# A Fourier layer folded by symmetry: map rows folded in the feed-forward before, tokens folded beside the root, the map ended half by half

## The chip, the cores and the metric

The kernel runs on one core of a Trainium2 chip. The metric is the device time of one execution in microseconds. Engines are named as in the profile: PE is TensorE (matmuls, with PEld its weight loads), DVE is VectorE, ACT is ScalarE, POOL is GpSimd, SP is SyncE, whose queue issues most DMAs.

## The reference

A two-layer encoder on 512 tokens of 1024 channels, in fp32. Layer 0 mixes tokens by differential attention and a gated linear recurrence; layer 1 by a Fourier transform. Each mixer and each feed-forward stands between two RMS norms:

```python
def fourier_mixer(h, w):
    B, S, D = h.shape
    g = h.astype(jnp.float32).reshape(B, S, FOURIER_GROUPS, FOURIER_GROUP_DIM)
    f = jnp.fft.fft2(g, axes=(1, 3), norm='ortho').real
    return f.reshape(B, S, D).astype(h.dtype) @ w

def swiglu(h, wg, wu, wd):
    return (jax.nn.silu(h @ wg) * (h @ wu)) @ wd
...
    for l in range(DEPTH):
        ...
        x = x + rmsnorm(m, ln_mix_post[l])
        hn = rmsnorm(x, ln_ffn_pre[l])
        x = x + rmsnorm(swiglu(hn, w_ffn_gate[l], w_ffn_up[l], w_ffn_down[l]), ln_ffn_post[l])
```

There are 4 channel groups of 256 channels. The real part of a 2-D transform over positions and channels is cos(position) x cos(channel) - sin(position) x sin(channel), so both transforms are matmuls with constant matrices. `dft_pos` holds 257 cosine columns and 255 sine columns; `dft_ch` the cosine and sine matrix of one group.

## The kernel before

**Arithmetic.** Each fp32 operand is held as a high and a low part (`split`, L99 to L106: a cast on ScalarE, L103, then a subtraction on VectorE, L106). `mm3` (L108 to L111) multiplies two such pairs with three matmuls. Matmuls are 512 or about 256 columns wide.

**Weights.** All large weights are a list of 85 units of 1 MB, read in order by SP as two 512 KB halves into three raw buffers (`raw`), cast and split into pairs (`whi`, `wlo`) by `prep_half`. Units 48 to 51 are the Fourier layer's map, 52 to 84 the second feed-forward: 52 gate, 53 up, 54 gate, 55 up, and so on. For units in `LO_POOL` GpSimd, not VectorE, makes the low part. `next_unit(ahead)` hands out a unit and prepares those up to `ahead` further. A raw buffer is free for the next load when its low part is made. All pairs, activations and constants share 33 tiles of 4 KB a partition (tag `t`); when none is free, the instruction that would fill one waits for the last reader of an older one. PSUM has 8 banks of 512 columns.

**Stages.** Layer 0's mixer, its feed-forward (`ffn(0, ...)`), the Fourier layer, the second feed-forward. `ffn` runs 11 passes u, each with a gate and an up unit (`col_tiles`, matmuls `pc`), then the down projection `proj_tok` (matmuls `pj`), which takes the pairs of gated activations (`gs`) as moving operand and finishes the four blocks of 128 tokens one after the other; its last six pairs of weights a token are 36 matmuls. `finish` normalises a block while TensorE is at the next: `post_norm` (sum of squares on ScalarE, a one-column power on GpSimd, multiply-adds on VectorE), then `after`.

**The Fourier layer before.** `after0` calls `pre_norm_tok`: the root mean square (`pre_stats`), then high and low part of the whole normalised block (L788, L789), token rows on partitions. `load_dft`, a hook in the down projection, loads `dft_pos` on GpSimd's queue into 8 half tiles. `pos_dft(c, ks)` transforms over positions for one of 8 blocks of 128 channels (`put`, 12 matmuls of 512); the first six blocks run with the first three tokens, then take the fourth. The channel gain is applied as the result is split (`u`, L836, L837). `ch_dft(c)` transforms over channels (`pe`, `po`, 12 matmuls of about 256 a block), and `mirror` makes the full 512 positions from the even and odd half (L864, L865). The map is a `proj_tok` over 8 blocks of rows (192 matmuls of 512), whose `fin1` finishes a token block as its columns are done; `turn_x` transposes the normalised block and splits it into `hnhi`, `hnlo` for the feed-forward. The transposes of the last two blocks are put off into the feed-forward's first pass (`deferred`), which runs 256 tokens at a time (`halves`).

**Order.** Each engine runs its instructions in the order in which they stand in its queue, and waits at the first whose operands or buffers aren't ready. That order is fixed when the kernel is built, by a scheduler that mostly follows the order of the code.

## Time and profile before

| | |
|---|---|
| time, median of 3 runs | 1051.09 us (1050.26 to 1052.09) |
| the profiled execution's own time | 1050.92 us |
| its span | 1049.1 us |
| mean granted TensorE clock | 0.994 |
| PE busy | 1031.0 us (98%) |
| DVE, ACT, POOL busy | 477.8, 382.1, 96.2 us |
| first matmul of the Fourier layer | 600.35 us after the span's start |
| first matmul of the feed-forward behind it | 679.00 us |

The span runs from the first to the last instruction of the profiled execution; its time also has what lies around the span. The marks are starts of single instructions in the timeline. A group of the profile names line, engine, operation, output and inputs, and shapes; behind the bars stand busy time, the mean of one in ns, and the idle time of the engine ahead of it with what ended it. Line numbers are those of the kernel before, unless a row is from the changed one.

### The profile page before, as it was taken

The numbers are of one execution on the slowest core, as the hardware profiler recorded it, in microseconds if no ns is written. First come the engines' busy times: TensorE is split into PE (matmuls) and PEld (weight loads), VectorE is DVE, ScalarE is ACT, GpSimd is POOL, SyncE is SP. The second block draws the span as 40 slices with busy tenths as digits, with TensorE's granted clock in tenths as the row PEclk, the third lists the DMA queues.
The fourth block names the chain that finished last, engine by engine and source line by source line (L and its number), as shares of the span: only waits on it lengthen the run. The fifth ranks groups of instructions, "written<-read, shape, count | busy, mean of one in ns | idle before, by whom it ended". The sixth has DMA issues, their size and how long they took to land.

```text
span 1049.1 us, 12316 instructions
## 1 busy us (share of the span) xinstructions
PE 1031.0 (98%) x4959; PEld 857.8 (82%) x4959; DVE 477.8 (46%) x723; ACT 382.1 (36%) x629; POOL 96.2 (9%) x94
## 2 busy tenths in 40 slices
...
GB/s 224 124 93 115 104 41 81 143 19 63 234 105 111 120 90 81 81 119 82 141 142 80 3 88 131 6 89 207 113 115 93 81 81 120 81 80 138 3 1 81
DMA packets 72982, 102.41 MB, mean 98 GB/s; under 512 B 3879, under 2 KB 61276, under 8 KB 72925
## 3 DMA queue, kind: packets, MB, share of 16 engines
...
q10 hardware_dynamic: 578, 1.05, 0.3%
...
## 4 chain that ended last, share of the span: by engine, by line
PE 88%; DVE 6%; ACT 3%; issue 1%; DMA 1%; POOL 1%; SPq 0%; POOLq 0%; DVEq 0%; ACTq 0%
PE pc L110 15%; PE pc L109 15%; PE pc L111 15%; PE pj L111 10%; PE pj L110 10%; PE pj L109 10%; DVE p L588 1%; DVE p L582 1%; ACT whi L103 1%; PE pT L251 1%; ACT p L93 1%; PE pqk L109 1%; DVE aT L106 1%; DMA raw<-in_w_in_dram 1%; PE put L109 1%
## 5 line engine op out<-in xcount | busy, mean ns | idle before, releaser
L106 DVE TENSOR_TENSOR wlo<-raw,whi 128x1024 fp32r<-128x1024 f32 x158 | 192.2, 1241 | 273.1 <-ACT whi L103 222.0
L110 PE MATMUL pc<-hnlo,whi 128*128 128x512 f32 (+1 forms) x768 | 285.1, 372 | 0.0
L109 PE MATMUL pc<-hnhi,whi 128*128 128x512 f32 (+1 forms) x768 | 284.6, 372 | 0.5 <-ACT hnhi L103 0.5
L111 PE MATMUL pc<-hnhi,wlo 128*128 128x512 f32 (+1 forms) x768 | 284.9, 371 | 0.0
L103 ACT CAST whi<-raw 128x1024 fp32r<-128x1024 f32 x164 | 167.9, 1050 | 117.5 <-PE pj L110 31.1
L110 PEld LDWEIGHTS pc<-hnlo,whi 128*128 128x128 f32 x768 | 144.7, 188 | 25.5 <-DVE hnlo L106 0.4
L109 PEld LDWEIGHTS pc<-hnhi,whi 128*128 128x128 f32 x768 | 144.2, 188 | 26.0 <-ACT hnhi L103 1.0
L111 PEld LDWEIGHTS pc<-hnhi,wlo 128*128 128x128 f32 x768 | 144.7, 188 | 24.6
L109 PE MATMUL pj<-whi,gs 128*128 128x512 f32 x352 | 136.9, 389 | 0.0
L110 PE MATMUL pj<-wlo,gs 128*128 128x512 f32 x352 | 136.9, 389 | 0.0
L111 PE MATMUL pj<-whi,gs 128*128 128x512 f32 x352 | 136.9, 389 | 0.0
L93 ACT ACTIVATE gated<-pc 128x512 f32<-128x512 f32 x44 | 26.2, 597 | 271.8 <-PE pc L111 271.8
L749 DVE TENSOR_TENSOR gated<-gated,pc 128x512 f32<-128x512 f32 x44 | 30.2, 687 | 112.7 <-PE pc L111 112.7
L109 PEld LDWEIGHTS pj<-whi,gs 128*128 128x128 f32 x352 | 66.1, 188 | 13.8
L111 PEld LDWEIGHTS pj<-whi,gs 128*128 128x128 f32 x352 | 66.1, 188 | 13.7
L110 PEld LDWEIGHTS pj<-wlo,gs 128*128 128x128 f32 x352 | 66.1, 188 | 13.6
L217 POOL TENSOR_TENSOR r<-m,mhalf 128x1 f32<-128x1 f32 x32 | 17.5, 548 | 543.3 <-DVE m L216 536.8
L262 ACT ACTIVATE junk<-pj 128x512 f32<-128x512 f32 x32 | 19.2, 599 | 94.9 <-DVE y L261 57.8
L261 DVE TENSOR_TENSOR y<-pj,gpost 128x512 f32<-128x512 f32 x32 | 22.0, 689 | 56.6 <-PE pj L111 56.5
L103 ACT CAST gs<-gated 128x512 fp32r<-128x512 f32 x44 | 25.3, 618 | 52.1 <-PE pj L110 32.2
L106 DVE TENSOR_TENSOR gs<-gated,gs 128x512 fp32r<-128x512 f32 x44 | 28.4, 686 | 31.3 <-ACT gs L103 31.3
L93 ACT ACTIVATE p<-p,mn 128x512 f32<-128x512 f32 x32 | 22.9, 719 | 31.1 <-DVE mn L582 27.9
(193 smaller groups left out, 1261.2 us busy)
## 6 DMA issues: line engine op xcount, KB each, us to landing
raw<-in_w_ffn_gate_dram SPq DMA_DIRECT2D x44, 512.0 KB, 3.9
raw<-in_w_ffn_up_dram SPq DMA_DIRECT2D x44, 512.0 KB, 4.9
raw<-in_w_ffn_down_dram SPq DMA_DIRECT2D x44, 512.0 KB, 3.5
raw<-in_w_in_dram SPq DMA_DIRECT2D x20, 512.0 KB, 4.4
raw<-in_w_mix_out_dram SPq DMA_DIRECT2D x8, 512.0 KB, 3.3
raw<-in_w_fourier_out_dram SPq DMA_DIRECT2D x8, 512.0 KB, 3.7
pos<-in_dft_pos_dram POOLq DMA_DIRECT2D x8, 256.0 KB, 5.5
...
```

The lines of the kernel that those rows point to most:

```text
L93: ins = A.activation(out_, in_, func, **kw)
L103: A.copy(hi, src)
L106: lo_eng.tensor_tensor(out=lo, in0=src, in1=f(hi), op=ALU.subtract)
L109: T.matmul(ps, lhsT=l[0], rhs=r[0], start=start, stop=False)
L110: T.matmul(ps, lhsT=l[0], rhs=r[1], start=False, stop=False)
L111: T.matmul(ps, lhsT=l[1], rhs=r[0], start=False, stop=stop)
L217: G.tensor_tensor(out=r, in0=m, in1=mhalf[:, 0:1], op=ALU.pow)
L251: T.transpose(pt[:, k * P:(k + 1) * P], xh[:, k * P:(k + 1) * P], ident)
L261: V.tensor_tensor(out=ys[h], in0=ps[h], in1=g[:, h * S:(h + 1) * S], op=ALU.mult)
L262: A.activation(junk, ps[h], AF.Square, scale=RD, accum_out=ss[h])
L582: last_score[0] = V.tensor_tensor_reduce(out=pr[m], in0=ps[m], in1=bias[h][:, 384 - t * P:384 - t * P + S], op0=ALU.add, op1=ALU.min, scal ...
L749: V.tensor_tensor(out=gated[fc], in0=gated[fc], in1=ps, op=ALU.mult)
```

## The change

The Fourier layer is written anew around symmetries. With even and odd combinations of channels c and 256-c only half of the channel matrix is needed, and with even and odd combinations of the map's rows j and 256-j of each group the mirrored channel outputs never have to be made.

- **Tokens.** `pre_norm_tok` multiplies a block by the gain, adds and subtracts the reversed channels of each group, and scales the folded block by the root as it is split. The blocks 2 and 3 of x are stored to DRAM (`scratch`) and gathered back with reversed rows, since the second half of the tokens now comes out mirrored.
- **Map rows.** `fold_w`, called in passes 1 to 4 of layer 0's feed-forward, loads 128 rows of a group, gathers the reversed other half, adds and subtracts, and stores both to DRAM (`wfold`), from which units 48 to 51 are read.
- **The rest.** Channel 128 of each group goes through `pos_rest`, `ch_rest` and a row tile `w128`/`wr`; token 256 through `acc`, four multiply-adds with rows of `wfold`.
- **The transforms.** `pos_dft` works on halves of about 256 columns, `ch_dft` has 8 matmuls a group, the map 104 matmuls in two halves of the tokens (`map_part`, `map_rest`), each ended by `map_out`.
- **The feed-forward behind.** Its first pass (`wide`) takes three weight units (two passes' gate, one up) by halves of the tokens; the transposes of the last two blocks all come between the halves. Units 48, 50, 52 and 54 join `LO_POOL`.
- **The start and the end.** Index rows for the gathers are made on GpSimd at the start; two of the four output blocks go out by a scatter.

```diff
-LO_POOL = (8,9,10,11,12,13)
+LO_POOL = (8,9,10,11,12,13,48,50,52,54)
...
+    def fold_w(g):
+        a, b, c = (tile1k("fold") for _ in range(3))
+        nc.sync.dma_start(a, w_fourier_out[g * 256:g * 256 + P, :])
+        gather(b, w_fourier_out, rowx["w%d" % g])
+        G.memset(b[0:1, :], 0.0)
+        V.tensor_tensor(out=c, in0=a, in1=b, op=ALU.add)
+        V.tensor_tensor(out=a, in0=a, in1=b, op=ALU.subtract)
+        for z, w in enumerate((c, a)):
+            G.dma_start(wfold[g * 256 + z * P:g * 256 + (z + 1) * P, :], w)
...
-                    if deferred and (h == 1 or c == P):
+                    if deferred and (h == 1 or c == P) and not (late and h == 0):
                         deferred.pop(0)()
+                while late and deferred:
+                    deferred.pop(0)()
...
+        if wide:
+            ug, uu, vg = next_unit(2), next_unit(1), next_unit(0)
+            col_tiles([(ug, 0), (ug, P), (uu, 0), (uu, P), (vg, 0), (vg, P)],
+                      lambda i, ps: consume(i, ps, 0) if i < 4 else consume(i - 4, ps, 1), True, True)
+            vu = next_unit(3)
+            col_tiles([(vu, 0), (vu, P)], lambda i, ps: consume(i + 2, ps, 1), False)
...
     def pre_norm_tok(t):
+        r = pre_stats(t, [junk, junk])
+        h = tile1k("h")
+        V.tensor_tensor(out=h, in0=xt[t], in1=g_pre1[0], op=ALU.mult)
...
+        V.tensor_tensor(out=wv[:, 0, :, 1:P], in0=hv[:, :, 1:P], in1=hv[:, :, 255:P:-1], op=ALU.add)
+        V.tensor_tensor(out=wv[:, 1, :, 1:P], in0=hv[:, :, 1:P], in1=hv[:, :, 255:P:-1], op=ALU.subtract)
...
+        for z in range(2):
+            sl = slice(z * S, (z + 1) * S)
+            A.activation(hi[:, sl], w[:, sl], AF.Copy, scale=r)
+            V.scalar_tensor_tensor(out=lo[:, sl], in0=w[:, sl], scalar=r, in1=f(hi[:, sl]), op0=ALU.mult, op1=ALU.subtract)
...
     def after0(t):
...
+        if t >= 2:
+            nc.sync.dma_start(scratch[(t - 2) * P:(t - 1) * P, :], xt[t])
...
             posT.append([])
+            for z in range(2):
+                w = tile1k("pos", F32R)
+                G.dma_start(w[:, 0:257], dft_pos[z, k * P:(k + 1) * P, 0:257])
+                G.dma_start(w[:, 258:513], dft_pos[z, k * P:(k + 1) * P, 257:512])
...
+    w128 = tile1k("w128")
+    G.memset(w128, 0.0)
+    for q in range(3):
+        nc.sync.dma_start(w128[32 * q:32 * q + 4, :], w_fourier_out.rearrange("(g j) d -> g j d", j=256)[:, P, :])
+    wr = tile1k("wr", F32R)
+    A.copy(wr, w128)
...
+    for g in range(4):
+        pos_dft(g, (0, 1, 2))
+    pos_rest((0, 1, 2))
+    prep_one()
+    pos_rest((3,))
...
+    for g in range(4):
+        ch_dft(g)
+    ch_rest()
+    gather(xr[1], scratch, rowx["c"])
+    gather(xr[2], scratch, rowx["d"])
...
+    for g in range(4):
+        raw = raws.tile([P, 1024], F32, name=nm("raw"), tag="raw")
+        nc.sync.dma_start(raw, wfold[g * 256:g * 256 + P, :])
...
+            V.scalar_tensor_tensor(out=acc, in0=raw, scalar=e256[g], in1=acc, op0=ALU.mult, op1=ALU.add)
...
+    split(acch, accl, acc)
...
+    def map_out(i):
+        y = [pair("ya"), pair("yc")]
+        for h in range(2):
+            A.copy(y[0][h], psm[i][1][h])
+            V.tensor_tensor(out=y[1][h], in0=psm[i][0][h], in1=y[0][h], op=ALU.add)
+            V.tensor_tensor(out=y[0][h], in0=psm[i][0][h], in1=y[0][h], op=ALU.subtract)
+        for z in range(2):
+            t = (z, 3 - z)[i]
+            post_norm(t, y[z], g_post1, G if z else V)
+            pre_norm(t, g_fpre1)
...
+    wf = [next_unit(2)]
+    for i in range(2):
+        for h in range(2):
+            map_part(i, h, 0)
+    wf += [next_unit(2), next_unit(2), next_unit(2)]
+    for h in range(2):
+        for g in (1, 2, 3):
+            map_part(0, h, g)
+        map_rest(0, h)
+    map_out(0)
...
+    turn_x(0)
+    turn_x(1)
+    map_out(1)
+    deferred.extend((lambda: turn_x(2), lambda: turn_x(3)))
...
-    ffn(1, after1, 4)
+    ffn(1, after1, 4, wide=True)
```

Where instructions now stand. First GpSimd's queue around the last token block of layer 0's feed-forward; `r` is the root of a mean square, `ch` the channel matrix. Before:

```order
78 L217 TENSOR_TENSOR r_4699<-m_4698,mhalf 128x1
79 L116 DMA gpre_5103<-in_ln_ffn_pre_dram 128x1024
80 L217 TENSOR_TENSOR r_4750<-m_4749,mhalf 128x1
81 L819 DMA ch_4769<-in_dft_ch_dram 128x1024
82 L217 TENSOR_TENSOR r_4763<-m_4762,mhalf 128x1
83 L819 DMA ch_4771<-in_dft_ch_dram 128x1024
84 L217 TENSOR_TENSOR r_5232<-m_5231,mhalf 128x1
85 L217 TENSOR_TENSOR r_5245<-m_5244,mhalf 128x1
```

After; `wlo` are low parts of unit 48, `x_816` and `x_817` the gathered blocks, `w_818` is w128:

```order
164 L117 DMA gpost_5181<-in_ln_mix_post_dram 128x1024
165 L251 TENSOR_TENSOR r_4898<-m_4897,mhalf 128x1
166 L117 DMA gpre_5183<-in_ln_ffn_pre_dram 128x1024
167 L251 TENSOR_TENSOR r_4910<-m_4909,mhalf 128x1
168 L107 TENSOR_TENSOR wlo_4928<-raw_4925,whi_4927 128x1024
169 L199 DMA x_816_4937<-scratch,ixc 128x1024
170 L107 TENSOR_TENSOR wlo_4934<-raw_4931,whi_4933 128x1024
171 L945 MEMSET w_818_4939 128x1024
172 L199 DMA x_817_4938<-scratch,ixd 128x1024
```

The memset of w128 stands behind both low parts and the first gather, where before only DMA issues stood behind the last root. Next ScalarE's queue at the same place, from the last block's squares on. Before, with `hnhi` the last block's high part and `u` the split position transforms:

```order
340 L223 ACTIVATE junk_4756,ss_4757<-x_82 128x512
341 L223 ACTIVATE junk_4756,ss_4758<-x_82 128x512
342 L788 ACTIVATE hnhi_4562<-x_82,r_4763 128x1024
343 L836 ACTIVATE u_4836<-put_4773,vcols 128x512
344 L836 ACTIVATE u_4842<-put_4783,vcols 128x512
345 L836 ACTIVATE u_4848<-put_4793,vcols 128x512
346 L836 ACTIVATE u_4854<-put_4803,vcols 128x512
347 L836 ACTIVATE u_4860<-put_4813,vcols 128x512
```

After, with `wr_4944` the cast of w128 and `whi_5036`, `whi_5042` the halves of unit 49:

```order
336 L257 ACTIVATE junk,ss_4904<-x_84 128x512
337 L257 ACTIVATE junk,ss_4905<-x_84 128x512
338 L104 CAST whi_4927<-raw_4925 128x1024
339 L104 CAST whi_4933<-raw_4931 128x1024
340 L846 ACTIVATE hnhi_4688<-w_4916,r_4910 128x512 x2
341 L949 CAST wr_4944<-w_818_4939 128x1024
342 L104 CAST whi_5036<-raw_5034 128x1024
343 L104 CAST whi_5042<-raw_5040 128x1024
344 L104 CAST u_5049<-put_5024 128x258
345 L104 CAST u_5058<-put_4948 128x512
346 L104 CAST u_5067<-put_4967 128x512
347 L104 CAST u_5076<-put_4986 128x512
```

Between the last block's high part and the first u now stand the cast of w128 and two weight casts. Last, ScalarE's queue at the end of the map. Before, with `pj` the map's sums and `whi` the weights of units 52 and 53:

```order
377 L103 CAST f_5093<-oy_5066 128x512
378 L103 CAST f_5098<-oy_5088 128x512
379 L103 CAST whi_5165<-raw_5163 128x1024
380 L103 CAST whi_5171<-raw_5169 128x1024
381 L103 CAST whi_5183<-raw_5181 128x1024
382 L103 CAST whi_5189<-raw_5187 128x1024
383 L262 ACTIVATE junk,ss_5224<-pj_5107 128x512
384 L262 ACTIVATE junk,ss_5225<-pj_5108 128x512
```

After, with `pm` the map's sums, `acc` the values of token 256, `whi_5215` to `whi_5257` units 50 and 51, `whi_5263` to `whi_5281` units 52 and 53:

```order
357 L992 CAST fr_4947<-pe_5164 128x256
358 L104 CAST acc_5201<-acc_5187 128x1024
359 L104 CAST whi_5215<-raw_5213 128x1024
360 L104 CAST whi_5221<-raw_5219 128x1024
361 L104 CAST whi_5251<-raw_5249 128x1024
362 L104 CAST whi_5257<-raw_5255 128x1024
363 L104 CAST whi_5263<-raw_5261 128x1024
364 L104 CAST whi_5269<-raw_5267 128x1024
365 L104 CAST whi_5275<-raw_5273 128x1024
366 L104 CAST whi_5281<-raw_5279 128x1024
367 L1043 COPY ya_5327<-pm_5207 128x512
368 L1043 COPY ya_5327<-pm_5208 128x512
```

All four casts of the feed-forward's weights, and ahead of them the casts of acc and the map's own, stand in front of the two copies that begin the first half's output.

More of the change, by code (lines that the diff above doesn't have):

```diff
@@ L188, in prep_one @@
         prep_half()
+    last_unit = [len(units)]
     def next_unit(ahead=3):
@@ L192, in next_unit @@
         consumed[0] += 1
-        while emitted[0] <= i + ahead and emitted[0] < len(units):
+        while emitted[0] <= i + ahead and emitted[0] < last_unit[0]:
             prep_one()
@@ L736, in drain, with ffn @@
         count[0] += 1
-    def ffn(l, after, tail, hook=None):
+    def ffn(l, after, tail, hook=None, wide=False, early=None):
         gated = [None] * NF
@@ new lines, in encoder_kernel, with pos_dft @@
+    last_unit[0] = len(units) - 4 - NF // 2 * 3
+    ffn(0, after0, 6, load_dft, early=lambda u: fold_w(u - 1) if 0 < u < 5 else None)
+    last_unit[0] = len(units)
+    prep_one()
+    xr = [xt[0], xpool.tile([P, D], F32, name=nm("x2"), tag="x2"), xpool.tile([P, D], F32, name=nm("x3"), tag="x3"), xt[1]]
+    ups = {}
+    def pos_dft(g, ts):
+        if g not in ups:
+            ups[g] = bank("put")
+        ps = ups[g]
+        for t in ts:
+            for z, (r0, o0, n) in enumerate(((0, 0, 258), (257, 256, 256))):
+                o = (z * 4 + g) * P
+                mm3(ps[:, o0:o0 + n], [a[:, o:o + P] for a in hf[t]], [a[:, r0:r0 + n] for a in posT[t]],
+                    t == 0 and z == 0, t == 3 and z == 1, skip_group_check=True)
@@ new lines, in pos_rest, with take_u @@
+    def pos_rest(ts):
+        if "r" not in ups:
+            ups["r"] = bank("put")
+        ps = ups["r"]
+        for t in ts:
+            mm3(ps[:, 0:258], [a[:, S:2 * S:4] for a in hf[t]],
+                [a[:, 0:258] for a in posT[t]], t == 0, t == 3)
+    uts = {}
+    def take_u(g):
+        uts[g] = pair("u", F32R)
+        split(*uts[g], ups[g])
+    w128 = tile1k("w128")
+    G.memset(w128, 0.0)
+    for q in range(3):
+        nc.sync.dma_start(w128[32 * q:32 * q + 4, :], w_fourier_out.rearrange("(g j) d -> g j d", j=256)[:, P, :])
@@ new lines, in encoder_kernel @@
+    wr = tile1k("wr", F32R)
+    A.copy(wr, w128)
+    V.tensor_tensor(out=wr[32:64, :], in0=w128[32:64, :], in1=f(wr[32:64, :]), op=ALU.subtract)
+    fr = tile1k("fr", F32R)
+    for g in range(4):
+        pos_dft(g, (0, 1, 2))
+    pos_rest((0, 1, 2))
+    prep_one()
+    pos_rest((3,))
+    uts["r"] = pair("u", F32R)
+    split(*[a[:, 0:258] for a in uts["r"]], ups["r"][:, 0:258])
+    for g in range(4):
+        pos_dft(g, (3,))
+        take_u(g)
+    fe, fo, e256 = [None] * 4, [None] * 4, {}
@@ new lines, in ch_dft @@
+    def ch_dft(g):
+        pe, po = bank("pe"), bank("po")
+        ut, ur = uts[g], uts["r"]
+        mm3(pe[:, 0:258], (chw(0), chw(1)), [a[:, 0:258] for a in ut], True, False)
+        for a in ur:
+            T.matmul(pe[:, 0:258], lhsT=chw(4 + g), rhs=a[:, 0:258], start=False, stop=a is ur[1])
+        mm3(po[:, 0:256], (chw(2), chw(3)), [a[:, 256:512] for a in ut], True, True)
+        eo = tile1k("feo", F32R).rearrange("p (n k) -> p n k", k=256)
+        e, o = fe[g], fo[g] = (eo[:, 0, :], eo[:, 1, :]), (eo[:, 2, :], eo[:, 3, :])
+        split(*[a[:, 0:256] for a in e], pe[:, 0:256])
+        e256[g] = sm("e256")
+        V.tensor_copy(e256[g], pe[:, 256:257])
+        for a in o:
+            G.memset(f(a[:, 0:1]), 0.0)
+        split(*[a[:, 1:256] for a in o], po[:, 1:256])
@@ new lines, in ch_rest @@
+    def ch_rest():
+        ps = bank("pe")
+        n = 0
+        for g in (0, 1, 2, 3, "r"):
+            for a in uts[g]:
+                T.matmul(ps[:, 0:258], lhsT=chw(8 + (4 if g == "r" else g)), rhs=a[:, 0:258], start=n == 0, stop=n == 9)
+                n += 1
+        e256["r"] = sm("e256")
+        V.tensor_copy(e256["r"], ps[:, 256:257])
+        A.copy(fr[:, 0:256], ps[:, 0:256])
+        V.tensor_tensor(out=fr[64:P, 0:256], in0=ps[64:P, 0:256], in1=f(fr[64:P, 0:256]), op=ALU.subtract)
@@ L876, in encoder_kernel @@
+    for g in range(4):
+        ch_dft(g)
+    ch_rest()
+    gather(xr[1], scratch, rowx["c"])
+    gather(xr[2], scratch, rowx["d"])
     g_post1 = gbc(ln_mix_post, 1, "gpost")
```

171 lines of the change are left out of this document (94 added, 77 removed).

## The prediction

> **What bounds the kernel now.** I read the page first: the busy shares and the chain of work that ended last.
>
> ```profile
> PE 1031.0 (98%) x4959; PEld 857.8 (82%) x4959; DVE 477.8 (46%) x723; ACT 382.1 (36%) x629; POOL 96.2 (9%) x94
> ...
> PE 88%; DVE 6%; ACT 3%; issue 1%; DMA 1%; POOL 1%; SPq 0%; POOLq 0%; DVEq 0%; ACTq 0%
> ```
>
> TensorE is busy 98% of the span and holds 88% of the chain. Then the stage that is rewritten: the waits of TensorE from 560 to 760 us, and its busy time by stage (columns: length, then busy time and instructions of PE, PEld, DVE, ACT, POOL, then clock, DMA share, GB/s).
>
> ```profile
> PE pc L109 <- ACT hnhi L103: 0.2, 1, 0.2
> ...
> 560.00:600.35 40.35, 40.35 (x180) 33.42 (x178) 18.00 (x34) 14.47 (x34) 3.27 (x6) 1.00 0.09 32
> 600.35:633.66 33.31, 33.31 (x193) 29.52 (x192) 20.43 (x35) 18.32 (x35) 2.76 (x5) 1.00 0.30 86
> 633.66:677.20 43.54, 43.54 (x203) 36.21 (x202) 25.57 (x49) 18.19 (x42) 3.27 (x6) 1.00 0.21 68
> ```
>
> In 200 us TensorE waits 0.2 us. From 600.35 to 677.20 it is never idle, while VectorE is busy 20.43 + 25.57 = 46 of 77 us. So before, this stage is worth what its matmuls cost. Their paces and the marks of the stage, from the timeline (start, duration):
>
> ```profile
> 600.35 0.39 PE L109 MATMUL put<-pos,hnhi 128*128 128x512 f32 x1
> 600.58 0.39 PE L110 MATMUL put<-pos,hnhi 128*128 128x512 f32 x1
> ...
> 679.00 0.28 PE L109 MATMUL pc<-hnhi,whi 128*128 128x256 f32 x1
> 679.11 0.28 PE L110 MATMUL pc<-hnlo,whi 128*128 128x256 f32 x1
> 679.23 0.28 PE L111 MATMUL pc<-hnhi,wlo 128*128 128x256 f32 x1
> ...
> 731.93 0.60 ACT L93 ACTIVATE gated<-pc 128x512 f32<-128x512 f32 x1 [5.28 <-PE pc L111]
> ```
>
> A 512-wide matmul takes 0.2267 us (0.23, to more places over a run of them), a 256-wide one 0.12. The layer starts at 600.35, the next feed-forward at 679.00, and that one's third pair of weights (u=2) at 731.93 less 24 x 0.2267 = 726.5.
>
> **The change part by part.** *TensorE's own work.* Before: 96 + 192 matmuls 512 wide and 96 about 256 wide: 288 x 0.2267 + 96 x 0.12 = 76.8 us. After: 96 + 12 + 42 about 256 wide and 104 of 512: 150 x 0.12 + 104 x 0.2267 = 41.6. The wide first pass adds 96 matmuls of 0.12 and drops 48 of 0.2267: +0.6. If TensorE never waited, the change would be worth -34.6 us. The question is how much of that becomes waiting. I follow the waits link by link in the order the changed program has, on the clock of before, with these durations (VectorE, ScalarE and GpSimd groups with their mean ns; then DMA landings):
>
> ```profile
> L106 DVE TENSOR_TENSOR wlo<-raw,whi 128x1024 fp32r<-128x1024 f32 x158 | 192.2, 1241 | 273.1 <-ACT whi L103 222.0
> L103 ACT CAST whi<-raw 128x1024 fp32r<-128x1024 f32 x164 | 167.9, 1050 | 117.5 <-PE pj L110 31.1
> L217 POOL TENSOR_TENSOR r<-m,mhalf 128x1 f32<-128x1 f32 x32 | 17.5, 548 | 543.3 <-DVE m L216 536.8
> L262 ACT ACTIVATE junk<-pj 128x512 f32<-128x512 f32 x32 | 19.2, 599 | 94.9 <-DVE y L261 57.8
> L261 DVE TENSOR_TENSOR y<-pj,gpost 128x512 f32<-128x512 f32 x32 | 22.0, 689 | 56.6 <-PE pj L111 56.5
> L103 ACT CAST gs<-gated 128x512 fp32r<-128x512 f32 x44 | 25.3, 618 | 52.1 <-PE pj L110 32.2
> L106 DVE TENSOR_TENSOR gs<-gated,gs 128x512 fp32r<-128x512 f32 x44 | 28.4, 686 | 31.3 <-ACT gs L103 31.3
> ...
> L106 POOL TENSOR_TENSOR wlo<-raw,whi 128x1024 fp32r<-128x1024 f32 x12 | 29.2, 2441 | 26.8 <-ACT whi L103 26.8
> L494 POOL TENSOR_TENSOR gate<-gate,xc 128x512 f32<-128x512 f32 x8 | 12.3, 1560 | 40.0 <-ACT gate L93 40.0
> ...
> L532 POOL TENSOR_TENSOR gate<-gate,gate 128x512 f32<-128x512 f32 x4 | 5.4, 1346 | 17.6 <-DVE c L586 17.6
> L810 POOL DMA_DIRECT2D pos<-in_dft_pos_dram x4 | 2.1, 537 | 0.0
> masks.py:197 POOL MEMSET ident<- 128x128 f32 x1 | 0.2, 206 | 0.3 <-POOLq L935 0.3
> L935 POOL MEMSET const-float32-1.0<- 128x1 f32 x1 | 0.1, 99 | 0.0
> ...
> raw<-in_w_ffn_gate_dram SPq DMA_DIRECT2D x44, 512.0 KB, 3.9
> raw<-in_w_ffn_up_dram SPq DMA_DIRECT2D x44, 512.0 KB, 4.9
> raw<-in_w_fourier_out_dram SPq DMA_DIRECT2D x8, 512.0 KB, 3.7
> raw<-in_w_mix_out_dram SPq DMA_DIRECT2D x8, 512.0 KB, 3.3
> out_dram<-x SPq DMA_DIRECT2D x4, 256.0 KB, 2.0
> vrows<-in_conv_w_dram SPq DMA_DIRECT2D x1, 8.0 KB, 4.4
> ```
>
> *In layer 0's feed-forward.* The folds add 8 VectorE adds of 1.24 (10 us over four passes) and GpSimd DMAs to engines that are mostly idle there: nothing; without that cover, 10 us. The eight wider position tiles take shared tiles in the down projection. In three places a pair of activations is now split one or two matmuls ahead of its use: 0.62 + 0.69 less that cover leaves about 0.7, three times: **+2.2** (0 to 3.9).
>
> *The wait for row 128 (w128).* The last token's statistics stand here before:
>
> ```profile
> 602.90 1.41 DVE L266 SCALAR_TENSOR_TENSOR x<-y,r,x 128x512 f32<-128x512 f32 x2 [0.69 <-POOL r L217]
> ...
> 605.42 0.56 POOL L217 TENSOR_TENSOR r<-m,mhalf 128x1 f32<-128x1 f32 x1 [2.02 <-DVE m L216]
> ```
>
> The gain multiply (1.24) now stands ahead of that m on VectorE, and the folds make a token cost VectorE slightly more than the 36 x 0.2267 = 8.16 us in which TensorE makes one (0.2): the pow ends at 605.42 + 0.56 + 1.24 + 0.2 = 607.4. Behind it GpSimd has a weight's low part (2.44), the gather of a row-reversed token, another low part (2.44), and the 128x1024 memset. The memset's price is 0.1 + 8 x 0.1 = 0.9 from the two memset rows. The gather has no row: its issue is between 0.5 (the plain DMA) and 2.4 (the longest row); 1.0, nearer the plain DMA. So the memset ends at 614.2. Only then may SP's three small loads go; they land after 2.0 to 4.4, I take the middle, 3.2: 617.4. ScalarE holds the cast wr for that, and behind it, in order, stand two weight casts and all casts of u: 1.05 + 2 x 1.05 + about 1.0 gives the first group's u at 621.6, and its low part, behind wr's and two weights' on VectorE, at 623.3. TensorE's 108 position matmuls end at 600.35 + 108 x 0.12 = 613.3. It idles 8.3 us, then 1.6. The 42 channel matmuls end at 623.3 + 5.0 = 628.3.
>
> *The clock after an idle stretch.* The trace has one such stretch (layer 0), in the timeline and in windows:
>
> ```profile
> 175.61 0.39 PE L110 MATMUL poT<-aT,v 128*128 128x256 f32 x1 [3.02 <-DVE aT L106]
> ...
> 176.00:179.00 3.00, 3.00 (x16) 2.67 (x17) 1.95 (x8) 2.13 (x6) 0.00 (x0) 0.51 0.38 145
> 179.00:182.00 3.00, 3.00 (x15) 2.19 (x16) 2.46 (x6) 2.51 (x5) 1.53 (x1) 0.92 0.01 3
> ```
>
> After 3.02 us without a matmul the granted clock is 0.51 and 0.92: 3 x 0.49 + 3 x 0.08 = 1.7 us lost. The idle 8.3 us will do the same, on the path: **+1.7**. The later idle stretch before the feed-forward does it too, but the waits inside that pass take it up. A third gap, of about 3 us (below), lies at this row's length: by the row another 1.7 (1059.4), which I leave to the range since transposes run in it. The Trainium skill, page "TensorE: Matmul & The Clock Gate", section "What's actually happening", puts the change to half clock after an idle window of some 3.4 us; by it that third gap is free and the sum stays 1057.7. The trace's 3.02 us speaks for an earlier point.
>
> *The map.* All four products with token 256's values (acc) wait for the last channel matmul. From 628.3 one chain runs through the three raw buffers: a multiply 1.24, a load into the freed buffer 3.7, two multiply-adds 2 x 1.24, acc's cast and a weight's cast 2.1, two GpSimd low parts 4.9 (units 50 and up are now GpSimd's), a load 3.9, cast 1.05, GpSimd 2.44, a load 4.9, cast 1.05: 27.8 us, to 656.1, about 0.4 more with issue times: 656.5. ScalarE's copies that begin the first half's output stand behind that last cast, which serves the next layer. TensorE's 104 matmuls need 23.6 us, wait 4.4 in between and end at about 656.3.
>
> *The first half's output.* From 656.5: copies and adds 3, squares 1.6, m and pow 0.8, x 1.4, squares 1.4, pow 0.9 (behind token 1's two multiplies, 2 x 1.56, on GpSimd), normalised token 1.4: 667.0. Token 1 repeats all from its squares on, 7.0, of which 0.5 overlaps; turned and split, 1.3. The feed-forward's first matmul comes at **674.8**, after 18.5 us with little but transposes; before, 679.00.
>
> *The wide pass.* 288 x 0.12 = 34.6. Its third pair's weights (unit 54) are cast behind the second half's activations on ScalarE and GpSimd: waits of about 2.8 + 2.0 + 1.3 = 6.1. Tokens 2 and 3 are then turned all at once, uncovered: 3. So it ends at 718.5; 48 x 0.2267 = 10.9 for unit 55 gives 729.4 for u=2, against 726.5: **+2.9**. Start (index rows, under an idle GpSimd) and scattered output: nothing (up to 1).
>
> **The sum:** 2.2 + 1.7 + 2.9 = +6.8 on the profiled execution's 1050.92 us (span 1049.1, 1.8 around it), 0.17 under the median shown: **1057.7 us**. The waits are 2.2 + 9.9 + 1.7 + 4.4 + 18.5 + 9.1 = 45.8 us, against the 34.6 saved and 4.5 of transposes and small waits that before has between the same marks beside its matmuls.
>
> **The rivals.**
> 1. *The wide pass doesn't wait* (faster). If unit 54's casts slip ahead of their use, 9 us go: 1048.7. It decides on unit 54: with under 2.3 us of waits in that pass the time equals before's. Against: its casts stand behind the second half's on two engines in order. For: the first half's chain may be late, and then the second half's matmuls are all done. Chance 0.12.
> 2. *All waits at their low ends*: no wide-pass waits (9), none in the feed-forward of layer 0 (2.2), the small loads after 2.0 and the gather 0.5 (1.7), the map's three loads after 3.3 (2.6), GpSimd's multiplies 1.35 (0.4): 1041.8. For: VectorE has slack in every window above. Against: the chains go by order, not by load. Chance 0.20.
> 3. *Longer waits*: the small loads take 4.4 (1.2), the gather 2.4 (1.4), a third clock loss (1.7), another 1.5 in the map: 1063.5. Chance 0.14.
> 4. *TensorE keeps its 98%*: 1016.3. The orders on ScalarE speak against it. Chance 0.03.
>
> **How the numbers follow.** Forecast 0.45 (its own range 1052 to 1063); the four rivals 0.49; 0.06 for a sum that comes to nothing. A measurement of this kernel tells 0.2%, 2.1 us, from no change. Faster: rivals 2 and 4 and two thirds of 1: 0.31. Same: the rest of 1 and the nothing, 0.09. Slower: 0.60. The range runs from rival 2 to rival 3, 1041 to 1064.
>
> **What would show it.** Right: a wait of TensorE near 613 us for u that the trace puts down to ScalarE, of 8 to 10 us, with wr's cast just before; a clock near 0.5 after it; ScalarE's copies of the map directly behind the cast of an up weight; some 18 us of idle before the first pc matmul; waits in the wide pass for ScalarE and GpSimd. Wrong: u cast before 616, the copies before 650, or a wide pass of under 37 us.

## The result, and the profile after

The changed kernel takes 1065.86 us (median of 4 runs, 1065.57 to 1067.09) against 1051.57 for the kernel before: a ratio of 1.0140, interval 1.0125 to 1.0155, some 14.3 us slower. The forecast was 1057.7 us, 6.6 over the median shown there. The direction is right; the forecast change is less than half of the measured one. Of the times below, that of experiment 2 leaves out one execution of 2033.85 us, far from the other three.

The page of the changed kernel, busy shares and chain:

```profile
PE 1011.1 (95%) x4877; PEld 841.3 (79%) x4877; DVE 500.4 (47%) x741; ACT 378.5 (36%) x621; POOL 165.0 (15%) x217
...
PE 77%; DVE 11%; ACT 4%; POOL 3%; issue 3%; DMA 1%; POOLq 0%; DVEq 0%; SPq 0%; ACTq 0%
```

TensorE is busy 20 us less in a span that is 16 us longer, and its share of the chain has gone from 88% to 77%: VectorE, ScalarE and GpSimd now hold most of what it gave up. Where TensorE waits, from 440 to 760 us:

```profile
PE pT L285 <- DVE xn L277: 15.5, 2, 11.6
PE pe L110 <- ACT u L104: 9.0, 1, 9.0
PE pc L110 <- ACT whi L104: 2.4, 1, 2.4
PE pm L111 <- POOL wlo L107: 2.2, 2, 1.1
PE pj L110 <- ACT gs L104: 2.0, 3, 1.0
PE pc L112 <- POOL wlo L107: 1.7, 1, 1.7
PE pT L285 <- DVE hnlo L107: 1.0, 1, 1.0
...
```

Before, the same window held 0.2 us. The places that the prediction named are in this list: the wait for u (L104) behind w128, the map (`pm`), the first half's output (`pT`), unit 54 in the wide pass (`pc`), the pairs of activations in layer 0 (`pj`) and the second half's transposes. The marks, from TensorE's timeline:

```profile
604.27 0.28 PE L110 MATMUL put<-pos,hnhi 128*128 128x258 f32 x1
...
628.52 0.58 PE L110 MATMUL pe<-u,ch 128*128 128x258 f32 x1 [8.98 <-ACT u L104]
...
675.69 1.94 PE L285 MATMUL pT<-ident,xn 128*128 128x128 f32 x8 [11.61 <-DVE xn L277]
...
683.32 0.58 PE L110 MATMUL pc<-hnhi,whi 128*128 128x256 f32 x1
...
699.08 0.39 PE L110 MATMUL pc<-hnhi,whi 128*128 128x256 f32 x1 [2.40 <-ACT whi L104]
...
701.52 0.58 PE L112 MATMUL pc<-hnhi,wlo 128*128 128x256 f32 x1 [1.70 <-POOL wlo L107]
...
730.19 0.40 PE L110 MATMUL pc<-hnhi,whi 128*128 128x512 f32 x1
...
1056.39 0.39 PE L112 MATMUL pj<-whi,gs 128*128 128x512 f32 x1
```

The wide pass ends at 730.19; unit 55's 48 matmuls of 0.2267 us bring u=2, the start of the third pair of weights, to 741.1. The profiled execution took 1067.09 us, 1.2 over its median; its span of 1065.3 is 16.2 longer than before's 1049.1. By stage:

| stage | before | after | change | forecast |
|---|---|---|---|---|
| up to layer 0's down projection | 480.7 | 481.2 | +0.5 | 0 |
| that down projection | 119.7 | 123.1 | +3.4 | +2.2 |
| Fourier layer, to the first pc matmul | 78.65 | 79.05 | +0.4 | -2.5 |
| from there to u=2 | 47.5 | 57.8 | +10.3 | +7.1 |
| u=2 to the last matmul | 315.1 | 315.3 | +0.2 | 0 |
| from the last matmul's start to the span's end | 7.5 | 8.9 | +1.4 | 0 |

Inside the Fourier layer the forecast's parts compare so: first position matmul to first channel matmul 24.25 (forecast 21.25), channel matmuls 8.9 (8.4), from there to ScalarE's copies 26.1 (28.2), copies to first pc matmul 19.8 (18.3). The wide pass took 46.9 (43.7). The forecast column has the clock's +1.7 in the Fourier layer.

### The profile page after: what moved, and what is told of

It reads as the page before. It is cut to its first block, busy times and chain, and to the rows that moved or that the text cites. A ratio compares the mean times of both kernels' runs of the same rounds, so it can differ in the third digit from the quotient of the medians.

```text
span 1065.3 us, 12346 instructions
## 1 busy us (share of the span) xinstructions
PE 1011.1 (95%) x4877; PEld 841.3 (79%) x4877; DVE 500.4 (47%) x741; ACT 378.5 (36%) x621; POOL 165.0 (15%) x217
## 4 chain that ended last, share of the span: by engine, by line
PE 77%; DVE 11%; ACT 4%; POOL 3%; issue 3%; DMA 1%; POOLq 0%; DVEq 0%; SPq 0%; ACTq 0%
PE pc L112 15%; PE pc L110 15%; PE pc L111 15%; PE pj L110 8%; PE pj L112 8%; PE pj L111 8%; DVE x L300 1%; POOL wlo L107 1%; ACT whi L104 1%; DVE p L623 1%; DVE p L617 1%; PE pT L285 1%; ACT p L94 1%; PE pqk L110 1%; PE pqk L111 1%
## 5 line engine op out<-in xcount | busy, mean ns | idle before, releaser
L107 DVE TENSOR_TENSOR wlo<-raw,whi 128x1024 fp32r<-128x1024 f32 x150 | 186.1, 1264 | 243.6 <-ACT whi L104 192.5
L110 PE MATMUL pc<-hnhi,whi 128*128 128x512 f32 (+1 forms) x784 | 288.8, 371 | 2.7 <-ACT whi L104 2.4
L112 PE MATMUL pc<-hnhi,wlo 128*128 128x512 f32 (+1 forms) x784 | 289.6, 370 | 1.7 <-POOL wlo L107 1.7
L111 PE MATMUL pc<-hnlo,whi 128*128 128x512 f32 (+1 forms) x784 | 289.2, 370 | 0.0
L104 ACT CAST whi<-raw 128x1024 fp32r<-128x1024 f32 x164 | 168.2, 1049 | 135.6 <-DMA raw<-in_w_ffn_gate_dram 45.9
L110 PEld LDWEIGHTS pc<-hnhi,whi 128*128 128x128 f32 x784 | 149.2, 191 | 28.0 <-ACT whi L104 2.6
L112 PEld LDWEIGHTS pc<-hnhi,wlo 128*128 128x128 f32 x784 | 149.7, 191 | 26.5 <-POOL wlo L107 1.9
L111 PEld LDWEIGHTS pc<-hnlo,whi 128*128 128x128 f32 x784 | 149.7, 191 | 24.4 <-DVE hnlo L107 0.2
L94 ACT ACTIVATE gated<-pc 128x512 f32<-128x512 f32 x44 | 26.1, 597 | 240.2 <-PE pc L112 240.2
L107 POOL TENSOR_TENSOR wlo<-raw,whi 128x1024 fp32r<-128x1024 f32 x20 | 48.3, 2425 | 61.2 <-ACT whi L104 61.1
L104 ACT CAST gs<-gated 128x512 fp32r<-128x512 f32 x44 | 25.3, 618 | 73.7 <-PE pj L111 52.0
L296 ACT ACTIVATE junk<-pj 128x512 f32<-128x512 f32 x24 | 14.3, 597 | 74.5 <-DVE y L295 53.4
L295 DVE TENSOR_TENSOR y<-pj,gpost 128x512 f32<-128x512 f32 x24 | 16.4, 687 | 48.2 <-PE pj L112 48.2
```

What stands on the lines that cost most here:

```text
L94: ins = A.activation(out_, in_, func, **kw)
L104: A.copy(hi, src)
L107: lo_eng.tensor_tensor(out=lo, in0=src, in1=f(hi), op=ALU.subtract)
L110: T.matmul(ps, lhsT=l[0], rhs=r[0], start=start, stop=False, **kw)
L111: T.matmul(ps, lhsT=l[0], rhs=r[1], start=False, stop=False, **kw)
L112: T.matmul(ps, lhsT=l[1], rhs=r[0], start=False, stop=stop, **kw)
```

## The experiments

Each was timed against the kernel before, and its ratio is to that one; a ratio of 0.001 is 1.05 us. The runs come from several chips, so a gain is the difference of two ratios; differences of the medians stand within 1.7 us of it. An interval reaches 1 to 2 us to either side, so gains of 3 us and less are weak where I don't say that their intervals are apart. Experiments 1, 2, 3 and 14 are edits of the changed kernel (1.0140).

### 1. w128 zeroed and loaded early

```diff
     def load_dft():
         calls[0] += 1
+        if calls[0] == 88:
+            w128s.append(tile1k("w128"))
+            G.memset(w128s[0], 0.0)
+            for q in range(3):
+                nc.sync.dma_start(w128s[0][32 * q:32 * q + 4, :], ...)
...
-    w128 = tile1k("w128")
-    G.memset(w128, 0.0)
...
```

> The zeroing and the three small loads of w128 are put into the down projection of layer 0's feed-forward (at the hook's 88th call), some 16 us before they are needed; the cast wr stays where it is in ScalarE's queue. Theory 1 (the changed kernel's 9.0 us wait of the first channel matmul for u is the wait for w128): wr no longer waits, and the next thing late is the second half of unit 49, whose load needs the raw buffer that GpSimd's low part of unit 48 frees at about 614.8; with a landing of 4.5 the first u is cast at about 621.5 instead of 628.4. TensorE then idles about 2 us instead of 9, the clock stays at 1.0 through the channel matmuls, the stage ends about 9.7 us earlier, and all of it reaches the end: about 1056 us. Rival (the map's weights are late anyway, since the stage behind is bound by loads through three raw buffers): the wait reappears in front of the map, and the time falls by less than 4 us, to 1062 or more.

Measured: 1058.77 us, ratio 1.0064 (1.0048 to 1.0081), 8.0 us less. In the changed kernel GpSimd's queue, then ScalarE's cast, read:

```profile
611.41 1.06 POOL L251 TENSOR_TENSOR r<-m,mhalf 128x1 f32<-128x1 f32 x1
612.45 2.38 POOL L107 TENSOR_TENSOR wlo<-raw,whi 128x1024 fp32r<-128x1024 f32 x1
615.00 1.31 POOL L199 DMA_INDIRECT x<-scratch,ixc  x1 [0.18 <-issue]
616.35 2.41 POOL L107 TENSOR_TENSOR wlo<-raw,whi 128x1024 fp32r<-128x1024 f32 x1
618.68 0.97 POOL L945 MEMSET w<- 128x1024 f32 x1
...
624.77 1.04 ACT L949 CAST wr<-w 128x1024 fp32r<-128x1024 f32 x1 [10.93 <-DMA w<-in_w_fourier_out_dram]
```

That is the forecast queue, instruction for instruction. ScalarE waits 10.9 us for the three small loads before it can begin the cast. In the experiment, ScalarE and TensorE at the same place:

```profile
613.64 1.03 ACT L953 CAST wr<-w 128x1024 fp32r<-128x1024 f32 x1
614.58 1.04 ACT L104 CAST whi<-raw 128x1024 fp32r<-128x1024 f32 x1
618.17 1.05 ACT L104 CAST whi<-raw 128x1024 fp32r<-128x1024 f32 x1 [2.55 <-DMA raw<-wfold]
619.12 2.32 ACT L104 CAST u<-put 128x258 fp32r<-128x258 f32 x5
...
620.03 0.39 PE L110 MATMUL pe<-u,ch 128*128 128x258 f32 x1 [0.59 <-ACT u L104]
```

The wait of 8.98 us is 0.59. The next thing late is unit 49's load, as expected, 2.4 us sooner than expected. The gain reaches the end, so this wait was on the path; the rival's bound of 4 us is out. It is less than the 9.7 us expected, and one part of the expectation failed: the clock did not stay at 1.00 in the channel matmuls. It was 0.61 from 622 to 625, after this wait and one of 1.61 us for u's low part. That low part stood on VectorE behind those of two weights and of `wr`, and the one of `wr` took 3.77 us beside GpSimd, where it had taken 1.22 in the changed kernel with GpSimd idle:

```profile
615.96 3.77 DVE L954 TENSOR_TENSOR wr<-w,wr 32x1024 fp32r<-32x1024 f32 x1
616.24 2.40 POOL L107 TENSOR_TENSOR wlo<-raw,whi 128x1024 fp32r<-128x1024 f32 x1
```

### 2. Matmuls that nothing reads, in that wait

```diff
+    pd = bank("pd")
+    for n in range(60):
+        T.matmul(pd[:, 0:258], lhsT=hf[3][0][:, 0:P], rhs=posT[3][0][:, 0:258], start=True, stop=True)
```

> Sixty matmuls of 258 columns are added behind the position transform, into a spare PSUM bank that nothing reads; they take 60 x 0.12 = 7.2 us of the 9.0 us in which TensorE waits for w128. No wait is taken away. Theory 1 (the lost clock behind the wait is on the path): the clock stays at 1.0 in the channel matmuls, which are then paced by VectorE's low parts of u, and end about 3 us earlier; total about 1063 us. Rival (the half clock is covered by the chain of casts and loads behind it): the clock is full and the time is the same, 1065 to 1067.

Measured: 1063.64 us (the median of 1063.61, 1063.64 and 1065.82), ratio 1.0130 (1.0110 to 1.0150). By windows, with the clock in the third column from the right, first the changed kernel, behind the wait for w128 and behind the waits of the wide pass:

```profile
628.50:632.00 3.50, 3.21 (x11) 2.62 (x12) 3.50 (x6) 1.72 (x4) 0.00 (x0) 0.50 0.74 184
632.00:635.50 3.50, 3.50 (x18) 3.50 (x18) 2.32 (x9) 1.95 (x6) 0.00 (x0) 0.50 0.28 116
635.50:639.00 3.50, 3.50 (x24) 3.23 (x23) 2.53 (x8) 1.12 (x4) 0.00 (x0) 0.96 0.02 5
...
701.50:704.50 3.00, 2.98 (x14) 2.98 (x14) 2.35 (x1) 0.00 (x0) 2.89 (x2) 0.50 0.55 159
704.50:707.50 3.00, 3.00 (x16) 3.00 (x16) 1.16 (x2) 0.00 (x0) 0.00 (x0) 0.51 0.61 180
707.50:710.00 2.50, 2.50 (x23) 2.50 (x23) 0.00 (x0) 0.00 (x0) 0.00 (x0) 1.00 0.07 20
```

Then the experiment:

```profile
627.50:630.00 2.50, 1.81 (x8) 1.23 (x9) 2.50 (x5) 1.42 (x3) 0.00 (x0) 1.00 0.68 211
630.00:633.00 3.00, 3.00 (x27) 3.00 (x26) 3.00 (x11) 2.27 (x7) 0.00 (x0) 1.00 0.57 173
```

The added matmuls keep the clock: from the first channel matmul to the first of the map (`pm`) 6.6 us pass instead of 8.9, 2.3 us less in the trace. The time falls by 1.1 us by the ratios, with intervals that overlap. That the idle stretch costs the clock is shown; that the clock is on the path here is seen in the trace alone, and the ratio lies between the theories.

### 3 and 4. Low parts by VectorE

Experiment 3 takes units 50, 52 and 54 from GpSimd; experiment 4 is 1 and 3 together.

```diff
-LO_POOL = (8,9,10,11,12,13,48,50,52,54)
+LO_POOL = (8,9,10,11,12,13,48)
```

> The low parts of units 50, 52 and 54 go back from GpSimd (2.43 us each) to VectorE (1.24 us); unit 48 stays with GpSimd. Theory 1 (the map's end waits for a chain of loads whose buffers GpSimd frees late): ScalarE's copies of the map start 3 to 4 us earlier than 663.6, and the wide pass waits for a low part 1.1 us less; about 1061 us, and 2.9 less again if the clock then stays up in the wide pass (1058). Rival (these low parts are off the path, the loads themselves at about 2.7 us each set the pace): copies at 663 and 1065 us or more.

> The first and the third experiment together: w128 early, units 50, 52 and 54 by VectorE. Theory 1 (one path, the two waits one behind the other): the gains add up, about 14 us, 1052 us, level with the kernel before. Rival (the two hide each other): no more than the larger of the two.

Measured: 1062.55 us, 1.0112 (1.0095 to 1.0129), 2.9 us less; and 1053.95 us, 1.0033 (1.0022 to 1.0045), 11.2 us less, about the sum of 8.0 and 2.9. Experiment 3's interval just overlaps that of the changed kernel; the sum supports its gain. ScalarE's copies start at 660.5 in experiment 3 (663.6 in the changed kernel). So the two waits lie one behind the other, and GpSimd's low parts are on the path. The gain is 2.9 where nearly 5 was expected (1061 us); that the loads through three raw buffers set the rest of the pace is my reading, which no run tested.

### 5, 6, 7 and 8. Order on ScalarE, unit 54, and the position tiles

All are edits of experiment 4's kernel (1.0033); experiment 8 holds all three.

```diff
 # 5
-    wf += [next_unit(2), next_unit(2), next_unit(2)]
+    wf += [next_unit(2), next_unit(1), next_unit(0)]
...
     map_out(0)
+    prep_one()
+    prep_one()
 # 6
+    prep_one()
     map_out(1)
 # 7
-        if k < 4 and calls[0] >= 32 + 4 * k:
+        if k < 4 and calls[0] >= 60 + 4 * k:
```

> On the fourth experiment's kernel (w128 early, units 50, 52, 54 by VectorE): units 52 and 53 are prepared behind the call that ends the first half of the map, not ahead of it, so that ScalarE's copies stand behind the map's own four weight casts and not behind the four of the next layer. In the fourth experiment the first half's sums are done at 646.5 and the copies start at 651.3. Theory 1 (order on ScalarE holds the end of the map): copies and first pc matmul 4.8 us earlier, 1049 us. Rival (the four casts, now in the middle of that end, take their 4.2 us there, or unit 52 comes late for the wide pass): first pc matmul no earlier than 670, or the gain is lost as waits of the wide pass; 1052 or more.

> On the fourth experiment's kernel: unit 54 is prepared ahead of the call that ends the second half of the map. Theory 1 (the wide pass waits 3.4 us for unit 54's cast, and the clock it loses there costs 2.9 more): no wait for a weight in the wide pass and a full clock in it; the turned tokens of the second half, whose norm is ready at about 691, then set the end of the first half pass and give about 2 us back: 1050 us. Rival (the second half's norm is the bound of the wide pass, the wait for the weight only lies in front of it): the wait moves to the transposes, 1053 or more.

> On the fourth experiment's kernel: the position tiles are loaded from the hook's 60th call on instead of the 32nd, when the down projection has begun to give tiles back. Theory 1 (three waits for a pair of activations in layer 0's down projection, 2.0 us, and the rest of its 3.4 us, come from the shared tiles that the eight position tiles hold): the waits go, the Fourier layer starts 2 to 3.4 us earlier, 1051 us. Rival (the added VectorE work per token makes the down projection longer): 1053.5 or more, with the same start.

> The fifth, sixth and seventh experiments together on the fourth's kernel. Theory 1 (waits one behind the other on one path): the gains add, about 10 us, 1043 to 1045 us, faster than the kernel before. Rival (the norm of the second half is the bound, and the others only feed it): 1049 or more.

Measured: experiment 5, 1051.84 us, 1.0005 (0.9995 to 1.0016), 2.9 less; experiment 6, 1049.78, 0.9991 (0.9982 to 1.0001), 4.4 less; experiment 7, 1051.73, 1.0008 (0.9999 to 1.0018), 2.6 less; experiment 8, 1047.85, 0.9964 (0.9953 to 0.9975), 7.3 less, where the three add up to 9.9. All four intervals lie clear of experiment 4's. In experiment 5 the copies now wait for their sums and not for ScalarE's queue:

```profile
647.76 0.59 ACT L1047 COPY ya<-pm 128x512 f32<-128x512 f32 x1 [2.81 <-PE pm L1041]
648.67 0.59 ACT L1047 COPY ya<-pm 128x512 f32<-128x512 f32 x1 [0.32 <-PE pm L1041]
```

In experiment 7 the Fourier layer starts at 601.37; its down projection takes 119.95 us, 119.7 in the kernel before: 3.1 of the 3.4 us there belong to the position tiles, and no matmul waits for a pair of activations any more. In experiment 6 no matmul of the wide pass waits for a weight. In experiment 8, all together, TensorE still waits 5.78 and 5.71 us for the first half's normalised tokens, and has one long wait left in the wide pass:

```profile
688.78 1.97 PE L285 MATMUL pT<-ident,xn 128*128 128x128 f32 x8 [5.02 <-DVE xn L277]
```

This is the second half's norm. These transposes come 20.7 us sooner than in the changed kernel (709.49), the end of the matmuls ahead of them nearly 26 us. The rival was right that the norm becomes the bound, and wrong that it does so at 1049.

### 9 and 14. The second block's multiplies on VectorE

Experiment 9 edits experiment 8's kernel, experiment 14 the changed kernel itself.

```diff
-            post_norm(t, y[z], g_post1, G if z else V)
+            post_norm(t, y[z], g_post1)
```

> On the eighth experiment's kernel: in the map's two ends the gain multiplies of the second token block go from GpSimd (two of 1.5 us) to VectorE (two of 0.68). Theory 1 (VectorE is held up while GpSimd reads two tensors: the two multiply-adds into x beside those multiplies took 3.42 us, elsewhere 1.41): they take 1.41 again, VectorE's two added multiplies lie in its wait for the next squares, each half's end gets 2 us shorter, and the first pc matmul and the last transposes come 2 and 2 to 4 us earlier: about 1045 us. Rival (the long multiply-adds have another cause, or the added 1.3 us of VectorE eat the gain): 1047 to 1048.

> The changed kernel with one edit: the second block's multiplies in the map's two ends on VectorE. Theory 1 (the prediction's 18.5 us for the first half's end left out that VectorE is held up beside GpSimd): the two multiply-adds into x take 1.4 instead of 3.4 us in both ends, the first pc matmul comes 2 us sooner after ScalarE's copies (17.8 instead of 19.8), the second end is 2 us shorter and with it unit 54's casts in the wide pass come earlier: 2 to 4 us in all, 1062 to 1064 us. Rival (the end is set by ScalarE's squares): 1065 to 1066.

Measured: experiment 9, 1045.19 us, 0.9947 (0.9934 to 0.9961), 1.8 us less than experiment 8; experiment 14, 1064.58, 1.0121 (1.0105 to 1.0136), 2.0 less than the changed kernel. Each interval overlaps that of the kernel it edits. In the changed kernel, VectorE's multiply-adds into x with GpSimd's multiplies (first and third row) and without:

```profile
669.69 3.42 DVE L300 SCALAR_TENSOR_TENSOR x<-y,r,x 128x512 f32<-128x512 f32 x2 [0.74 <-POOL r L251]
...
677.20 1.42 DVE L300 SCALAR_TENSOR_TENSOR x<-y,r,x 128x512 f32<-128x512 f32 x2 [0.66 <-POOL r L251]
...
669.64 2.93 POOL L295 TENSOR_TENSOR y<-yc,gpost 128x512 f32<-128x512 f32 x2
```

And in experiment 14, at the same place:

```profile
669.79 1.42 DVE L300 SCALAR_TENSOR_TENSOR x<-y,r,x 128x512 f32<-128x512 f32 x2 [0.74 <-POOL r L251]
```

The durations bear out theory 1: with GpSimd's multiplies gone the pair takes 1.42 us. The times speak for it too, two gains of the same size, at its lower end.

### 10 and 13. The clock in the wide pass's gap

Experiment 10 edits experiment 8's kernel; 13 is 9 and 10 together.

```diff
+                if late and deferred:
+                    for n in range(36):
+                        T.matmul(pss[5][:, 256:512], lhsT=wcol(...)[0], rhs=hns(n % KD, 0, 256)[0], start=True, stop=True)
                 while late and deferred:
                     deferred.pop(0)()
```

> On the eighth experiment's kernel: 36 matmuls of 256 columns (4.3 us) are added between the two halves of the wide pass, where TensorE waits 5.0 us for the second half's norm; they go into the unwritten half of a bank that the next pass begins anew, so no wait and no result changes. Theory 1 (the clock lost in that wait is on the path, since nothing late follows it): the clock stays at 1.0 after the transposes where it was 0.54 for 5 us, 2.3 us earlier: 1045.5 us. Rival (the clock falls all the same, or the time is covered): 1047.5 to 1048.5.

> The ninth and tenth experiments together on the eighth's kernel: the second block's multiplies on VectorE, and matmuls that nothing reads in the wait between the halves of the wide pass. Theory 1 (two terms of the sum, independent): the ratio to before of 0.9947 falls by the clock's 0.7 to 2.3 us to 0.993, about 1043.5 us. Rival (the shorter second half leaves a wait so short that the added matmuls themselves delay the next pass): 0.995 or more.

Measured: experiment 10, 1046.55 us, 0.9957 (0.9943 to 0.9971), 0.7 us less than experiment 8; experiment 13, 1043.60, 0.9934 (0.9920 to 0.9947), 1.4 us less than experiment 9 and faster than both kernels. The clock behind the gap, in experiment 8 and in experiment 10:

```profile
690.00:695.00 5.00, 4.45 (x22) 3.69 (x21) 2.77 (x4) 2.28 (x4) 0.00 (x0) 0.54 0.00 0
```

```profile
690.00:695.00 5.00, 4.23 (x29) 3.28 (x30) 3.32 (x5) 2.35 (x4) 0.00 (x0) 1.00 0.00 0
```

The clock holds each time. Each gain alone lies inside its intervals; three runs (2, 10, 13) give 1.1, 0.7 and 1.4 us in the same direction. I read a cost of about 1 us a gap, and not the 2.3 that the trace of one execution shows. Such a trace is one draw: after much the same waits in the channel matmuls (0.5 to 0.8, then 1.4 to 1.8 us) the clock stayed at 1.00 in experiments 4, 9 and 11, which took 7.8 us from the first channel matmul to the map, and fell to about 0.50 in experiments 1, 5, 6, 7, 8, 10, 12 and 13, which took 8.8 to 10.1.

### 11. A narrow first pass

```diff
-    ffn(1, after1, 4, wide=True)
+    ffn(1, after1, 4)
...
-            col_tiles(..., u == 0)
+            col_tiles(..., u == 0, u == 0 and l == 1)
```

> On the eighth experiment's kernel: the feed-forward's first pass takes two weight units, as before the change, with all transposes of the last two blocks between its halves; four tiles of 2.9 us instead of six cover the second half's norm. Theory 1 (the wide pass only serves as cover for that norm, which is late by itself): TensorE waits 5.8 us longer between the halves and saves the 0.6 us that the narrow matmuls cost: about 1053 us. Rival (the norm comes earlier when unit 54 isn't prepared ahead of it, so that the wide pass gains nothing): 1048.

Measured: 1051.93 us, 1.0009 (1.0000 to 1.0018), 4.7 us more than experiment 8. TensorE's wait there:

```profile
687.65 3.65 PE L285 MATMUL pT<-ident,xn 128*128 128x128 f32 x16 [10.62 <-DVE xn L277]
```

10.6 instead of 5.0 us: two tiles of 2.9 us less to cover the norm with, and the wait is 5.6 us longer. The wide pass is worth its cost, as cover for a norm that comes late.

### 12. Plain stores

```diff
-        if t in (1, 2):
-            G.indirect_dma_start(out=out, out_offset=rowx[("oc", "od")[t - 1]], in_=xt[t], in_offset=None)
-            return
-        r = t // 3 * P
+        r = t * P
```

> On the eighth experiment's kernel: all four output blocks are stored by plain DMAs, so that two blocks come out with their rows in reversed order and place; nothing else is changed. Theory 1 (the 1.4 us by which the changed kernel's span goes on longer after the last matmul, 8.5 us instead of 7.1, are the two scatters): 7.1 us again, 1046.4 us. Rival (the longer end has another cause, as the last plain store lands after the scatters): 8.5 us and 1047.8.

This kernel leaves out the reordering of two output blocks. Measured: 1047.95 us, 0.9975 (0.9964 to 0.9985), no less than experiment 8's 0.9964. Its last matmul starts at 1036.89 and its span ends at 1045.6, 8.7 us later, where the table has 7.5 before and 8.9 after. The scatters are not the cause of the longer end. It lies behind the issue of the last store: from there to the span's end 3.2 us pass before, 4.6 in the changed kernel and 4.4 here. What lengthens it stays open.

## Why the prediction was right in direction and wrong in size

**What held.** That the work saved on TensorE turns into waits, the places of these waits and what holds each: w128 behind GpSimd's memset and ScalarE's order (experiment 1, 8.0 us), the map's end behind GpSimd's low parts (3, 2.9 us) and behind the next layer's casts (5, 2.9 us), unit 54 in the wide pass (6, 4.4 us), the position tiles (7, 2.6 us). Rivals 1, 2 and 4 needed waits to be short or absent; those for w128, of the first half's output and in layer 0 stand at their forecast length or above it. The wide pass waits 4.1 us for weights and not 6.1, still more than the 2.3 that rival 1 allowed. Only the stretch of the map came near rival 2's low end, 26.1 us and not 28.2. Rival 3, longer waits, came nearest with 1063.5: two of the causes it named, the small loads and a third clock loss, are what happened. The chances for no change and for slower add up to 0.10 and 0.59, where the text has 0.09 and 0.60.

**The step that failed** is the sum: terms sized too small, together 9.4 of the 16.2 us between the two spans. By stretches the misses are +3.0 (the wait for w128), +0.5 (channel matmuls), -2.1 (from there to the copies), +1.5 (the first half's output), +3.2 (the wide pass, through the clock), +1.2 (layer 0) and +2.1 (start, end and the second feed-forward, put at nothing).

1. *The wait for w128*: 24.25 us from the first position to the first channel matmul, not 21.25. The pow came later (and took 1.06, not 0.56), the gather took 1.31 and not 1.0, and the three small loads ended 5.1 us after the memset, where I took 3.2 and gave 4.4 as the upper end. In SP's queue of the changed kernel they stand right behind a 512 KB load:

```profile
618.78 0.32 SPq L1013 DMA_DIRECT2D raw<-wfold  x1
619.68 0.94 SPq L947 DMA_DIRECT2D w<-in_w_fourier_out_dram  x3
```

   The longest landing of a small load in the trace of before (4.4) was no bound here. That the large load delayed them is argued, not shown; the second gather ran beside them too.

   That TensorE's idle time, 8.98 us, came near the forecast 8.3 is partly luck. The position matmuls took longer as well: the last of the 108 starts 15.0 us after the first, where all were to take 13.0, and this hid 2 us of the wait. The twelve of `pos_rest` start every 0.23 us and not every 0.12; their weight loads, which the code takes from every fourth column, last 0.33 us where the others last 0.19. So the work saved is nearer 33 than 34.6 us.
2. *The clock*: I put the second loss at nothing since waits in the wide pass would take it up, and a third into the range. The second did go that way: half clock to 686.9, 1.8 us lost, and 2.0 us less waiting for unit 54 than forecast. The third came, at 701.5, and lasted 6 us. In this trace it accounts for most of the wide pass's 3.2 us too many; no run filled this very gap, and in two others a filled gap was worth about 1 us (experiments 2, 10, 13). The row of 3.02 us of idle gave 1.7 us lost; after 8.98 us of idle the half clock lasted 7 us. The Trainium skill, page "TensorE: Matmul & The Clock Gate", section "What's actually happening", has full clock return after at least one busy window of some 3.4 us; the 6 and 7 us of this trace are up to twice that.
3. *VectorE beside GpSimd*: "x 1.4" in the map's end took 3.42 in the first half and 3.48 in the second; 2.0 us in time (experiment 14). The trace of before has it, and the prediction left it out: one instruction form in layer 0, on VectorE beside GpSimd's low parts and alone.

```profile
100.23 2.85 DVE L588 SCALAR_TENSOR_TENSOR p<-p,c 128x512 f32<-128x512 f32 x1
...
108.34 0.74 DVE L588 SCALAR_TENSOR_TENSOR p<-p,c 128x512 f32<-128x512 f32 x1
...
100.14 5.20 POOL L106 TENSOR_TENSOR wlo<-raw,whi 128x1024 fp32r<-128x1024 f32 x2
```

   The Trainium skill, page "GPSIMD Engine Reference", section "1. Specifications", has GpSimd share its SBUF interfaces with VectorE, in contention with VectorE instructions that read two SBUF operands. The trace agrees: 2.85 against 0.74 us, and in experiment 1 3.77 against 1.22, longer by 2.55 us beside a GpSimd instruction of 2.40: VectorE lost about as much as GpSimd took.
4. *Layer 0's down projection*: +3.4, not +2.2 (inside its bounds of 0 to 3.9). The mechanism was right (experiment 7).
5. *Start and end*: +0.5 and +1.4, which I put at nothing. The end is not the scatters (experiment 12); neither was found.

Against these stands one term too large: from the channel matmuls to the copies 26.1 us, not 28.2.

**Where the expected gain went.** In experiment 13 the waits for w128, unit 54 and the position tiles are gone, and the kernel is 6.9 us faster than before (0.66%), not 34.6. Its page and its waits from 600 to 770 us:

```profile
PE 1008.1 (97%) x4913; PEld 840.4 (81%) x4913; DVE 500.3 (48%) x751; ACT 378.4 (36%) x621; POOL 144.0 (14%) x207
```

```profile
PE pT L285 <- DVE xn L277: 9.9, 2, 5.7
PE po L110 <- DVE u L107: 1.7, 1, 1.7
PE pT L285 <- DVE hnlo L107: 1.0, 1, 1.0
```

TensorE is busy 22.9 us less than before, the added matmuls among its work, and waits 9.9 us for the normalised tokens at the end of the map's first half, which ending it half by half leaves without cover. Before, the same end lay beside the map's own matmuls, one block of tokens behind the other. By the marks its Fourier layer takes 62.5 us, 16.1 less than before, and the stretch from there to u=2 54.4, 6.9 more. The clock has a share in this too, in the channel matmuls and around the transposes of the first half:

```profile
619.00:624.50 5.50, 5.50 (x33) 5.50 (x34) 4.42 (x14) 2.87 (x8) 0.00 (x0) 0.69 0.63 235
653.10:664.00 10.90, 5.19 (x21) 4.35 (x22) 9.58 (x16) 7.25 (x12) 1.10 (x2) 0.50 0.36 97
```

I have not divided the rest of the missing gain among waits, transposes without cover and lost clock.
